# Four changes of order in a two-layer decoder: RG-LRU queues, PSUM banks of the last out-projection, and the weights of the attention layer's output

## The chip, the cores and the metric

The kernel runs on one core of a Trainium2 chip. Its time is device microseconds of one execution; the time before is the median of three runs, 1180.68 us (1180.13 to 1182.38). The five engines are called PE (TensorE, matmuls), DVE (VectorE), ACT (ScalarE), POOL (GpSimd) and SP (SyncE, which here issues the DMAs). Each works off its own queue in the order in which the program was laid out for it.

## The reference

The input is 1024 tokens of 1024 channels in float32. Two pre-norm residual layers follow each other, then a last RMS norm.

```python
def lru_mixer(h, w_in, conv_w, conv_b, wa, ba, wx, bx, a_param, w_out):
    u = h @ w_in
    xb, gate = u[..., :LRU_WIDTH], u[..., LRU_WIDTH:]          # 1536 each
    xc = causal_depthwise_conv(xb, conv_w, conv_b)             # 4 taps
    r = sigmoid(block_diag_linear(xc, wa, ba))                 # 12 blocks of 128
    i = sigmoid(block_diag_linear(xc, wx, bx))
    log_a = -8.0 * r * softplus(-a_param)
    a = exp(log_a)
    bterm = sqrt(-expm1(2.0 * log_a)) * (i * xc)
    hs = scan(a, bterm)                    # h_t = a_t * h_(t-1) + bterm_t
    return (hs * silu(gate)) @ w_out

def fox_mixer(h, w_in, b_f, w_out):        # 16 heads of 64, causal
    q, k, v, gate, f_logit = split(h @ w_in)
    cum = cumsum(log_sigmoid(f_logit + b_f))
    p = softmax(causal(q k' / 8 + cum_q - cum_k))
    return (p v * silu(gate)) @ w_out

for i in (0, 1):
    x = x + (lru_mixer, fox_mixer)[i](rms_norm(x, norm_g[i]), ...)
return rms_norm(x, final_g)
```

## The kernel before

Channels lie on the 128 partitions, tokens run along the free dimension, in two halves of 512. Every float32 matrix is split into a rounded part and a remainder (names ending in `h` and `l`), and each product is three matmuls: high by high, weight remainder by high, weight by remainder (lines 111 to 113). Weights come from memory into a tile `wf` (three buffers), ACT casts the rounded part (`wh`, line 75), POOL subtracts for the remainder (`wl`, line 86); `wh` and `wl` have four buffers each. PSUM has eight banks: two single ones of tag `g`, two of tag `O`, and two pairs of tag `S`.

The program is written as ordinary nested loops and generators. A scheduler simulates the engines with its own estimate of every duration, and puts an instruction on its engine's queue when it is ready in that simulation; among ready ones the one that was written (traced) first goes first. `tc.issue_after(ins)` adds an order to this: every instruction traced in its block that runs on the engine of `ins` comes behind `ins` in the queue. It makes nobody wait for a result.

The first layer goes over 12 blocks of 128 channels (`n`). Each makes 48 matmuls `ups` (the convolution's input), 48 `gps` (the gate branch) and 12 `gate` (the block-diagonal products). `conv(n)` scales `ups` into `us` on DVE (line 260), which frees the pair of banks, makes the first tap on ACT (`xc`, line 261) and three more on DVE (line 264), and splits the result (`xch` on ACT, `xcl` on DVE). `gates(n)` has four products in the two banks of tag `O`, each freed by a tanh on ACT (line 285): two into `th`, two into `ti`; `state[n]["last"]` is the last of them. `recur(n)` makes two more functions and a square on ACT (lines 310 to 312), a product on DVE (313), a square root on ACT (315, with a table load before it and one before the next tanh), products and the scan on DVE (314, 316, 317). `silu` and `outputs` finish the block (294 to 296, 325, and the split into `yh` and `yl`). In iteration `n` the order of the trace is: half of `ups` of `n`, gates of `n - 1`, outputs of `n - 2` (behind `last` already), the other half of `ups`, convolution of `n`, fill, `gps` of `n - 1`, silu and recurrence of `n - 1`, fill. Fill is the out-projection of two finished blocks (`project_out`): 16 units of six matmuls (8 row blocks `db` by two halves), each in one bank of tag `g` and added to the residual `x` on DVE (line 350). Eight units are taken in each iteration from 3 on, so eight of the last sixteen are left when the loop ends; these are drained after the last `gps`, ahead of the last recurrence. The last two blocks' out-projection (lines 429 to 431) uses the pairs of tag `S`.

The second layer goes over 16 heads. For each, `run` works off a string in which digits step the attention's generators and a dot steps the fill and a side list. From head 13 on the fill is `partial`: the output projection of the first six pairs of heads, 8 row blocks by two token halves, 18 matmuls per unit in a bank of tag `g`, added to the first layer's residual, which is loaded and stored again. Before it `load_y` loads the two halves' `y` and splits them (ACT and DVE). The side list of head 14 is `late`: it loads the weights of the last pair of heads and casts them (`woh`, `wol`) into the tiles of the keys and queries, which are free when head 15's loads (lines 566 to 574) have read them; then it loads the `y` of pair 6. Lines 655 and 656 are the logits for the softmax statistics, 660 and 663 their maximum (DVE) and exponentials (ACT); 722 and 723 are the logits for the weights, 756 and 757 the products with the values.

Of the kernel before, what the change touches and what calls it, by code (L numbers as in the profile page):

```python
# [2 lines left out]

# [1 line left out]

# [6 lines left out]
F32 = mybir.dt.float32  # L12
# [3 lines left out]
ALU = mybir.AluOpType  # L16
# [22 lines left out]
def trunk(ctx: ExitStack, tc: tile.TileContext, xt, w0, wg, wo0, pc, gn, w1, wv, wf, bf, wo1, out):  # L39
# [59 lines left out]
    def weights(src, parts=wpool, lo_eng=nc.gpsimd):  # L99

        for k in range(0, src.shape[1], 4):
            n = min(4, src.shape[1] - k)
            yield from split_weights([(src[:, k : k + n], slice(0, P))], (n, P), nc.scalar, lo_eng, parts)
# [13 lines left out]
    def drain(gen):  # L117
        for _ in gen:
            pass
# [44 lines left out]
    with ExitStack() as l0:  # L164
# [92 lines left out]
        def conv(n, ups):  # L257
            us, xc = long("us"), long("xc", bufs=2)
            for pt, cs in zip(ups, halves if len(ups) == 2 else (slice(0, SEQ),)):
                nc.vector.tensor_tensor(us[:, cs], pt, rs[:, cs], ALU.mult)  # L260
            nc.scalar.activation(xc, us, AF.Identity, bias=cb[:, n : n + 1], scale=cw[3][:, n : n + 1])
            for d in range(1, 4):
                w_ = cw[3 - d][:, n : n + 1]
                nc.vector.scalar_tensor_tensor(xc[:, d:], us[:, : SEQ - d], w_, xc[:, d:], ALU.mult, ALU.add)
            xh, xl = long("xch", F32R), long("xcl", F32R)
            to_hi(xh, xc, nc.scalar)
            to_lo(xl, xc, xh, nc.vector)
            wt = wpool.tile([P, 4, P], F32, tag="wf", name="wgf", bufs=3)[:, :2]
            nc.sync.dma_start(wt, wg[n])
            wgh = tmp.tile([P, 2, P], F32R, tag="wgh", name="wgh")  # L270
            wgl = tmp.tile([P, 2, P], F32R, tag="wgl", name="wgl")
            to_hi(wgh, wt, nc.vector)
            to_lo(wgl, wt, wgh, nc.vector)
            state[n] = dict(xc=xc, x=(xh, xl), w=(wgh, wgl))
# [24 lines left out]
        def recur(n, parts=(slice(0, SEQ),)):  # L299
            s = state[n]  # L300
            a, t = long("a", bufs=2), long("m2")
            s["a"] = a
            old = 0.0
            for cs in parts:
                th, ti = (z[:, cs] for z in s["t"])
                a_, t_, xc = a[:, cs], t[:, cs], s["xc"][:, cs]

                nc.scalar.activation(t_, th, AF.Tanh, bias=c2[:, n : n + 1], scale=c2[:, n : n + 1])  # L310
                nc.scalar.activation(a_, th, AF.Exp, bias=nc2[:, n : n + 1], scale=nc2[:, n : n + 1])
                nc.scalar.activation(th, a_, AF.Square)
                nc.vector.scalar_tensor_tensor(t_, th, 1.0, t_, ALU.add, ALU.mult)
                nc.vector.scalar_tensor_tensor(ti, ti, 1.0, xc, ALU.add, ALU.mult)
                nc.scalar.activation(t_, t_, AF.Sqrt, scale=1.0 / 16.0)
                nc.vector.tensor_tensor(ti, ti, t_, ALU.mult)
                nc.vector.tensor_tensor_scan(a_, a_, ti, old, ALU.mult, ALU.add)
                old = a[:, cs.stop - 1 : cs.stop]

        def outputs(n, parts=(slice(0, SEQ),), gate=itertools.repeat(None)):  # L320
            s = state.pop(n)
            y = tuple(ypool.tile([P, SEQ], F32R, tag=z, name=z) for z in ("yh", "yl"))
            for cs, _ in zip(parts, gate):
                a_ = s["a"][:, cs]
                nc.vector.tensor_tensor(a_, a_, s["sg"][:, cs], ALU.mult)
                yh, yl = (z[:, cs] for z in y)
                to_hi(yh, a_, nc.scalar)
                to_lo(yl, a_, yh, nc.vector if len(parts) > 1 else nc.gpsimd)
            ys.append(y)

        def out_weights(g, d0):

            wt = wpool.tile([P, 4, P], F32, tag="wf", name="wf", bufs=3)
            for j in range(2):
                nc.sync.dma_start(wt[:, 2 * j : 2 * j + 2], wo0[d0 + j, :, 2 * g : 2 * g + 2])
            hi = wpool.tile([P, 4, P], F32R, tag="wh", name="wh")
            lo = wpool.tile([P, 4, P], F32R, tag="wl", name="wl")
            to_hi(hi, wt, nc.scalar)
            to_lo(lo, wt, hi, nc.gpsimd)
            return [[(hi[:, 2 * j + i], lo[:, 2 * j + i]) for i in range(2)] for j in range(2)]  # L340

        def project_out(g):

            for d0 in range(0, KT, 2):
                for db, w in enumerate(out_weights(g, d0), d0):
                    for h, cs in enumerate(halves):
                        pt = ps.tile([P, HALF], F32, tag="g", name="ops")
                        gemm(pt, zip(w, [tuple(z[:, cs] for z in p) for p in ys[2 * g : 2 * g + 2]]))
                        x = xs[h][db]
                        nc.vector.tensor_tensor(x, x, pt, ALU.add)  # L350
                        yield
# [11 lines left out]
        for n in range(NB):  # L363
            wu = first[0] if n == 0 else list(weights(w0[n]))
            if n == 1:
                ups = both = [ps.tile([P, HALF], F32, tag="g", name="ups") for h in range(2)]
            else:
                ups = two_banks("ups")
                both = [ups.rearrange("p a b -> p (a b)")]
                ups = [ups[:, h] for h in range(2)]  # L370
            product(ups[0], 0, wu)
            if n == 0:
                gps = held[0] = two_banks("gps")
                product(gps[:, 0], 0, first[1])
                for _ in zip(split_x(1), square_x(1)):
                    pass
                done = rms_row(sums[0], rs[:, :HALF])[1]
            else:
                gates(n - 1)
                if n > 1:  # L380
                    with tc.issue_after(state[n - 1]["last"].ins):
                        outputs(n - 2)
            product(ups[1], 1, wu)
            if n == 0:
                product(gps[:, 1], 1, first[1])
                rms_row(sums[1], rs[:, HALF:])
                with tc.issue_after(done.ins):
                    softplus()
            conv(n, both)
            if n % 2 and n > 1:  # L390
                fill = itertools.chain(fill, project_out((n - 3) // 2))
            take(fill, 4)
            if n > 1:
                wn = list(weights(w0[NB + n - 1]))
                gps = held[n - 1] = two_banks("gps")
                for h in range(2):
                    product(gps[:, h], h, wn)
            if n:
                drain(silu(state[n - 1], held.pop(n - 1)))
                recur(n - 1)  # L400
            take(fill, 4)
        gates(NB - 1)
        wn = list(weights(w0[2 * NB - 1]))
# [1 line left out]
        for h in range(2):  # L405
            product(gps[:, h], h, wn)
        outputs(NB - 2)
        drain(fill)
        recur(NB - 1, halves)
        outputs(NB - 1, halves, silu(state[NB - 1], gps, halves))  # L410
# [53 lines left out]
    with ExitStack() as l1:  # L464
# [344 lines left out]

        def partial():  # L810

            for db in range(KT):
                w = list(weights(wo1[db, :, :6]))
                for c in range(2):
                    x = at.tile([P, HALF], F32, tag="xp", name="xp", bufs=3)
                    nc.sync.dma_start(x, x1d[c, :, db])
                    pt = ps.tile([P, HALF], F32, tag="g", name="ops1")
                    yield from gemm_steps(pt, zip(w, y1[c]))
                    nc.vector.tensor_tensor(x, x, pt, ALU.add)
                    nc.sync.dma_start(x1d[c, :, db], x)  # L820

        def final(c, q):

# [57 lines left out]

        def late():

            for half in range(2):
                wh, wl = (kqpool.tile([P, 8, P], F32R, tag=f"qk{p}{half}", name=f"wo{p}") for p in "hl")
                for b in range(2):
                    wt = wpool.tile([P, 4, P], F32, tag="wf", name="wf", bufs=3)
                    for d in range(2):
                        nc.sync.dma_start(wt[:, 2 * d : 2 * d + 2], wo1[half * 4 + b * 2 + d, :, 6:8])
                    sl = slice(4 * b, 4 * b + 4)  # L890
                    to_hi(wh[:, sl], wt, nc.scalar)
                    to_lo(wl[:, sl], wt, wh[:, sl], nc.gpsimd)
                    yield
                late_w.extend([(wh[:, 2 * d + k], wl[:, 2 * d + k]) for k in range(2)] for d in range(4))
            for c in range(2):
                load_y(c, [6])
                yield
# [125 lines left out]
```

## Time and profile before

| | |
|---|---|
| median of three runs | 1180.68 us |
| profiled execution | 1183.53 us |
| its span | 1181.8 us |
| mean granted TensorE clock | 0.985 |
| first layer | to about 465 us |
| second layer | from about 465 us |

The profile is of one execution. Engine rows give the start, the duration, the engine, the line, the operation, output and inputs, shapes and count; in brackets stands how long the engine had been idle and what ended that. Window rows give the length of a stretch and, for each engine, busy time and instructions, then the granted clock and the DMA share. Busy times of PE come from modelled ends of matmuls, so the distance from one start to the next says more than a duration.

### The profile page before, as it was taken

The page shows a single profiled execution, that of the slowest core. Times are in us where ns is not written, and L with a number is a line of the kernel's source. Part 1 is how long each engine was busy: PE and PEld are TensorE (multiplying, and loading weights), DVE is VectorE, ACT ScalarE, POOL GpSimd, SP SyncE. Part 2 cuts the span into 40 slices and gives each one's busy share as a digit, 9 for nine tenths or more (in the row PEclk, how much of TensorE's full clock was granted, in tenths as well). Part 3 has the DMA queues.
Part 4 walks back from the last instruction along what each step waited for, and adds up shares of the span by engine and source line. Part 5 has one row for each costly group of instructions (what it writes and reads, how often), then busy time and mean ns, then how long its engine had stood idle before and what let it go on. Part 6 is the DMA issues. An engine that isn't in the chain of part 4 may idle for free.

```text
span 1181.8 us, 15783 instructions
## 1 busy us (share of the span) xinstructions
PE 1142.6 (97%) x5653; PEld 954.9 (81%) x5653; DVE 808.6 (68%) x1237; ACT 589.0 (50%) x1010; POOL 415.2 (35%) x370
## 2 busy tenths in 40 slices
PE   9998999999999998999999999999999999998996
PEld 7786788888888875878888988889888898787896
DVE  7588855777565877865777646776567765575666
ACT  8386354354553644464554545554455444435343
POOL 1233342333342422442343332433434334144345
PEclk9999999999999999999999999999999999999996
DMA  6111111111211114143343414433234332756434
GB/s 207 50 40 40 50 54 41 49 58 32 58 40 55 54 62 160 52 117 90 82 125 82 109 54 99 114 77 99 64 90 108 90 82 59 197 148 198 143 115 142
DMA packets 63277, 105.94 MB, mean 90 GB/s; under 512 B 8856, under 2 KB 27928, under 8 KB 63200
## 3 DMA queue, kind: packets, MB, share of 16 engines
q1 hardware_dynamic: 63200, 104.95, 31.7%
q8 instruction: 44, 0.72, 0.2%
q14 instruction: 33, 0.27, 0.1%
HBM read 63.30 MB, written 16.45 MB: 67 GB/s over the span
## 4 chain that ended last, share of the span: by engine, by line
PE 79%; DVE 10%; issue 3%; ACT 3%; DMA 3%; POOL 1%; SPq 1%; DVEq 0%; ACTq 0%; POOLq 0%
PE gps L113 10%; PE gps L112 10%; PE gps L111 10%; PE ops L111 5%; PE ops L112 5%; PE ops L113 5%; PE ups L113 3%; PE ups L111 3%; PE ST L722 3%; PE ups L112 3%; PE O L757 3%; PE ST L723 3%; PE S L656 3%; PE S L655 3%; PE O L756 3%
## 5 line engine op out<-in xcount | busy, mean ns | idle before, releaser
L86 POOL TENSOR_TENSOR wl<-wf,wh 128x512 fp32r<-128x512 f32 (+2 forms) x154 | 227.6, 1485 | 457.2 <-ACT wh L75 420.5
L113 PE MATMUL gps<-hl,wh 128*128 128x512 f32 x576 | 227.8, 396 | 2.5 <-DVE hl L86 2.5
L111 PE MATMUL gps<-hh,wh 128*128 128x512 f32 x576 | 227.5, 395 | 2.0 <-ACT hh L75 2.0
L112 PE MATMUL gps<-hh,wl 128*128 128x512 f32 x576 | 227.5, 395 | 0.0
L663 ACT ACTIVATE S<-S,st 128x128 f32<-128x128 f32 (+7 forms) x128 | 91.5, 715 | 149.1 <-DVE st L660 147.1
L75 ACT CAST wh<-wf 128x512 fp32r<-128x512 f32 (+2 forms) x156 | 93.7, 606 | 105.8 <-issue 27.2
L113 PEld LDWEIGHTS gps<-hl,wh 128*128 128x128 f32 x576 | 108.9, 189 | 26.8 <-DVE hl L86 3.0
L111 PEld LDWEIGHTS gps<-hh,wh 128*128 128x128 f32 x576 | 109.1, 189 | 23.7 <-ACT hh L75 2.5
L112 PEld LDWEIGHTS gps<-hh,wl 128*128 128x128 f32 x576 | 109.0, 189 | 21.2 <-POOL wl L86 0.3
L81 DVE CAST ph<-p 128x512 fp32r<-128x512 f32 (+2 forms) x130 | 80.4, 630 | 65.6 <-POOL p L736 38.4
L86 DVE TENSOR_TENSOR pl<-p,ph 128x512 fp32r<-128x512 f32 (+2 forms) x130 | 117.0, 919 | 2.0
L660 DVE CUSTOM_DVE_ANT_0 S<-S,mask 128x128 f32<-128x128 f32 (+7 forms) x128 | 96.8, 759 | 19.5 <-PE S L656 18.7
L736 POOL TENSOR_SCALAR_AFFINE_SELECT p<-p 128x128 f32<-128x128 f32 (+1 forms) x128 | 48.9, 400 | 127.3 <-ACT p L731 75.8
L350 DVE TENSOR_TENSOR x<-x,ops 128x512 f32<-128x512 f32 x80 | 53.6, 681 | 41.2 <-PE ops L113 40.9
L111 PE MATMUL ups<-hh,wh 128*128 128x512 f32 x192 | 76.5, 399 | 2.6 <-DVE us L260 1.9
L112 PE MATMUL ups<-hh,wl 128*128 128x512 f32 x192 | 75.5, 393 | 0.7 <-POOL wl L86 0.7
L113 PE MATMUL ups<-hl,wh 128*128 128x512 f32 x192 | 75.9, 395 | 0.2
L519 PE MATMUL vps<-wh,hh 128*128 128x256 f32 (+1 forms) x256 | 73.0, 286 | 1.6 <-DVE fz L531 1.6
L728 ACT ACTIVATE p<-ST 128x512 f32<-128x512 f32 (+1 forms) x68 | 52.9, 787 | 40.3 <-PE ST L723 35.4
L521 PE MATMUL vps<-wl,hh 128*128 128x256 f32 (+1 forms) x256 | 72.8, 286 | 0.0
L520 PE MATMUL vps<-wh,hl 128*128 128x256 f32 (+1 forms) x256 | 72.2, 283 | 0.0
L655 PE MATMUL S<-T,U 128*128 128x256 f32 (+2 forms) x192 | 67.5, 354 | 1.7 <-ACT S L663 1.6
(196 smaller groups left out, 2604.2 us busy)
## 6 DMA issues: line engine op xcount, KB each, us to landing
wf<-in_w SPq DMA_DIRECT2D x100, 256.0 KB
wf<-in_wo SPq DMA_DIRECT2D x64, 128.0 KB
T<-qkh SPq DMA_DIRECT2D x28, 256.0 KB
U<-qkh SPq DMA_DIRECT2D x28, 256.0 KB
x<-in_xt SPq DMA_DIRECT2D x16, 256.0 KB
x1d<-x SPq DMA_DIRECT2D x16, 256.0 KB
wf<-in_wv SPq DMA_DIRECT2D x16, 256.0 KB
xp<-x1d SPq DMA_DIRECT2D x16, 256.0 KB
```

The costliest lines, as they stand in the source:

```text
L75: nc.scalar.copy(hi, src)
L81: eng.tensor_copy(hi, src)
L86: return eng.tensor_tensor(lo, src, f32(hi), ALU.subtract)
L111: nc.tensor.matmul(o, wh, xh[:, cs], start=i == 0, stop=False)
L112: nc.tensor.matmul(o, wl, xh[:, cs], start=False, stop=False)
L113: nc.tensor.matmul(o, wh, xl[:, cs], start=False, stop=i == len(pairs) - 1)
L519: nc.tensor.matmul(pt, xh, wh, start=k == 0, stop=False)
L520: nc.tensor.matmul(pt, xl, wh, start=False, stop=False)
L521: nc.tensor.matmul(pt, xh, wl, start=False, stop=k == KT - 1)
L655: nc.tensor.matmul(S[:, lo_:hi_], U[s][:, 0, qs], T[s][:, 0, lo_:hi_], start=True, stop=False)
L660: nc.vector.tensor_tensor_reduce(S[:, :n], S[:, :n], mask[:, SEQ - n :], -1.0, -NEG, ALU.add, ALU.min, accum_out=m)
L663: nc.scalar.activation(S[:, :n], S[:, :n], AF.Exp, bias=f32(m), scale=-1.0, accum_out=sums[:, i : i + 1])
```

## The change

It has four edits. None adds or removes arithmetic or a transfer.

1. `conv(n)` (for `n` of 1 and more) and `recur(n - 1)` in the loop are traced inside `issue_after` of the last tanh of block `n - 1`: their ACT instructions (the first tap, the rounded split; the functions, the square and the root) come behind all four tanh of that block in ACT's queue. The last block's recurrence, after the loop, is not wrapped.
2. In the eight units drained after the loop, those of odd row blocks take a pair of banks of tag `S` in place of two single ones of tag `g`.
3. `partial` takes its first four units as (row block 0, half 0), (1, 0), (0, 1), (1, 1); before it was (0, 0), (0, 1), (1, 0), (1, 1). Two row blocks' weights are then held at once.
4. `late` begins with four empty steps, so that everything in it is traced four dots later.

```diff
@@ project_out
             for d0 in range(0, KT, 2):
                 for db, w in enumerate(out_weights(g, d0), d0):
+                    wide = two_banks("ops") if held is None and db % 2 else None
                     for h, cs in enumerate(halves):
-                        pt = ps.tile([P, HALF], F32, tag="g", name="ops")
+                        if wide is None:
+                            pt = ps.tile([P, HALF], F32, tag="g", name="ops")
+                        else:
+                            pt = wide[:, h]
@@ the loop over n
-            conv(n, both)
+            with tc.issue_after(state[n - 1]["last"].ins) if n else nullcontext():
+                conv(n, both)
...
             if n:
                 drain(silu(state[n - 1], held.pop(n - 1)))
-                recur(n - 1)
+                with tc.issue_after(state[n - 1]["last"].ins):
+                    recur(n - 1)
...
         outputs(NB - 2)
+        held = None
         drain(fill)
@@ partial
-            for db in range(KT):
-                w = list(weights(wo1[db, :, :6]))
-                for c in range(2):
-                    x = at.tile([P, HALF], F32, tag="xp", name="xp", bufs=3)
-                    nc.sync.dma_start(x, x1d[c, :, db])
-                    pt = ps.tile([P, HALF], F32, tag="g", name="ops1")
-                    yield from gemm_steps(pt, zip(w, y1[c]))
-                    nc.vector.tensor_tensor(x, x, pt, ALU.add)
-                    nc.sync.dma_start(x1d[c, :, db], x)
+            ws = {}
+            for db, c in [(0, 0), (1, 0), (0, 1), (1, 1)] + [(db, c) for db in range(2, KT) for c in range(2)]:
+                if db not in ws:
+                    ws[db] = list(weights(wo1[db, :, :6]))
+                x = at.tile([P, HALF], F32, tag="xp", name="xp", bufs=3)
+                nc.sync.dma_start(x, x1d[c, :, db])
+                pt = ps.tile([P, HALF], F32, tag="g", name="ops1")
+                yield from gemm_steps(pt, zip(ws[db], y1[c]))
+                nc.vector.tensor_tensor(x, x, pt, ALU.add)
+                nc.sync.dma_start(x1d[c, :, db], x)
@@ late
+            yield from itertools.repeat(None, 4)
             for half in range(2):
```

More of the change, by code (lines that the diff above doesn't have):

```diff
@@ L1 @@
 import itertools
-from contextlib import ExitStack
+from contextlib import ExitStack, nullcontext
 import numpy as np
```

## The prediction

> **What bounds the kernel now.** I read the page's busy times first, then the table of windows stage by stage, then the timelines of the engines around each stretch in which TensorE (PE) loses time.
>
> ```profile
> PE 1142.6 (97%) x5653; PEld 954.9 (81%) x5653; DVE 808.6 (68%) x1237; ACT 589.0 (50%) x1010; POOL 415.2 (35%) x370
> ```
>
> ```profile
> core 0: us, PE busy (x) PEld busy (x) DVE busy (x) ACT busy (x) POOL busy (x), PEclk, DMA share, GB/s
> 60.00:97.00 37.00, 37.00 (x162) 29.84 (x160) 33.31 (x25) 27.41 (x31) 12.47 (x7) 1.00 0.17 54
> 97.00:116.00 19.00, 14.06 (x52) 9.85 (x51) 15.56 (x12) 16.60 (x18) 6.28 (x3) 0.91 0.05 13
> 116.00:420.00 304.00, 303.61 (x1315) 246.72 (x1314) 204.58 (x191) 149.87 (x176) 103.63 (x59) 1.00 0.16 48
> 420.00:430.00 10.00, 7.89 (x33) 5.79 (x33) 9.92 (x11) 1.91 (x4) 4.74 (x3) 1.00 0.25 79
> 1020.00:1032.00 12.00, 9.11 (x36) 7.20 (x35) 7.08 (x13) 6.34 (x13) 1.97 (x2) 0.86 0.67 186
> 1060.00:1077.00 17.00, 13.67 (x56) 10.63 (x55) 7.06 (x12) 7.41 (x15) 9.15 (x9) 0.90 0.81 221
> ```
>
> PE is the bound: it is busy 97% of the span, and the change removes no matmul. So only its pauses, and what the clock loses behind them, can be won. From 116 to 420 us there is nothing to win (303.61 of 304.00 busy); 1315 matmuls in 304.00 us are 0.231 us each, my unit below. The four other windows are the places that the four edits touch. From 97 to 116, 52 matmuls should take 12.0 us and take 19.0: **7.0 lost**. From 420 to 430, 33 should take 7.6: **2.4 lost**. From 1020 to 1032 PE pauses 2.89, and from 1060 to 1077 it is idle 17.00 - 13.67 = **3.3**.
>
> **The change part by part.**
>
> *Convolution and root behind the tanh.* In the stretch from 97 ScalarE (ACT) works off its queue in an order that starves PE:
>
> ```profile
> 94.16 0.69 ACT L285 ACTIVATE th<-gate,hba 128x512 f32<-128x512 f32 x1
> 97.50 1.24 ACT L261 ACTIVATE xc<-us,pct 128x1024 f32<-128x1024 f32 x1 [2.66 <-DVE us L260]
> 98.65 0.67 ACT L285 ACTIVATE th<-gate,hba 128x512 f32<-128x512 f32 x1
> 106.73 1.28 ACT L285 ACT_TABLE_LOAD   x1
> 108.02 0.69 ACT L285 ACTIVATE ti<-gate,hbx 128x512 f32<-128x512 f32 x1
> ```
>
> ```profile
> 99.37 0.50 PE L111 MATMUL gate<-xch,wgh 128*128 128x512 f32 x1 [2.01 <-ACT th L285]
> 108.76 0.50 PE L111 MATMUL gate<-xch,wgh 128*128 128x512 f32 x1 [2.21 <-ACT ti L285]
> 109.86 0.63 PE L111 MATMUL ops<-yh,wh 128*128 128x512 f32 x1
> ```
>
> The convolution of block 3 (xc at 97.50) stands between the two th of block 2 and waits 2.66 us for DVE; the second th, its bank full, waits behind it, and PE waits for the bank. At 108.76 the same happens with the last ti, behind a root and a table load. With the edges all four tanh go first, and neither pause can arise in this way: this is the 7.0, with the slow matmuls that follow (0.63 at 109.86). On the clock: behind the pause of 2.21 the rows are 0.63 long. [...]
>
> The price is paid earlier, where the convolution now runs ahead because ACT has nothing to do:
>
> ```profile
> 57.90 1.25 ACT L261 ACTIVATE xc<-us,pct 128x1024 f32<-128x1024 f32 x1 [0.29 <-DVE us L260]
> 68.74 1.04 ACT L75 CAST xch<-xc 128x1024 fp32r<-128x1024 f32 x1
> 69.68 0.69 ACT L285 ACTIVATE ti<-gate,hbx 128x512 f32<-128x512 f32 x1
> ```
>
> ```profile
> 59.18 4.83 DVE L264 SCALAR_TENSOR_TENSOR xc<-us,pct,xc 128x1023 f32<-128x1023 f32 x3 [0.18 <-ACT xc L261]
> 64.11 1.23 DVE L260 TENSOR_TENSOR us<-ups,rs 128x1024 f32<-128x1024 f32 x1
> 68.30 1.22 DVE L313 SCALAR_TENSOR_TENSOR m<-th,m 128x1024 f32<-128x1024 f32 x1 [2.96 <-ACT th L312]
> 70.10 1.22 DVE L86 TENSOR_TENSOR xcl<-xc,xch 128x1024 fp32r<-128x1024 f32 x1
> 72.77 1.23 DVE L316 TENSOR_TENSOR ti<-ti,m 128x1024 f32<-128x1024 f32 x1 [0.32 <-ACT m L315]
> 77.22 1.26 DVE L264 SCALAR_TENSOR_TENSOR xc<-us,pct,xc 128x1023 f32<-128x1023 f32 x1
> ```
>
> ```profile
> 67.68 0.39 PE L113 MATMUL gate<-xcl,wgh 128*128 128x512 f32 x1
> 73.43 0.39 PE L111 MATMUL gate<-xch,wgh 128*128 128x512 f32 x1
> ```
>
> Block 1's xc runs at 57.90, before block 0's tanh; it must now wait for their last. PE issues block 0's last gate product at 67.68, so, nothing else standing before it, that ti ends at about 68.9 and xc at 70.1. Queued behind the waiting xc is xch alone, but DVE needs it: three taps (4.83 at 59.18, or three of the single tap at 77.22, 3.8; I take 3.9) end at 74.0, m of the recurrence takes 1.2, xch 1.04 beside it, xcl 1.22, so block 1's gates start near 76.5 instead of 73.43. And us of block 2, which frees the two banks for ups of block 3, moves from 64.11 to 76.4. PE's other product, gps of block 1, has three matmuls left at 73.43, so without these gates it ends at 74.1. So I expect a **new pause of 2.4 us near 74**. Behind it the clock costs between nothing (the pause of 2.01) and 10 matmuls at 0.2 more (2.0, the pause of 2.21); I take 1.3. DVE, busy 33.31 of 37.00, has some 6 us less done by 70, which the 11 us of a later ups hide as long as its banks are free by 103. Sum: -7.0 + 2.4 + 1.3 = **-3.3**, bounds -7.0 (no new pause) and +8 (below).
>
> In the later blocks:
>
> ```profile
> 236.93 1.25 ACT L310 ACTIVATE m<-th,c 128x1024 f32<-128x1024 f32 x1
> 242.79 1.04 ACT L75 CAST yh<-a 128x1024 fp32r<-128x1024 f32 x1
> ```
>
> ```profile
> 247.61 3.20 DVE L317 TENSOR_TENSOR_SCAN a<-a,ti 128x1024 f32<-128x1024 f32 x1
> 261.73 2.24 DVE L325 TENSOR_TENSOR a<-a,sg 128x1024 f32<-128x1024 f32 x1
> ```
>
> The recurrence's first steps run between th and ti; behind the last ti (yh at 242.79 follows it) they start at most 5.9 later, and the scan ends by 256.7, where its reader starts at 261.73. xc, waiting for less, comes sooner. Cover 5.0 us; cost 0. Were it gone, each microsecond late would be one on POOL's yl and then on the products, which have eight units queued ahead.
>
> *Four banks for the last chain's products.*
>
> ```profile
> 424.09 0.67 DVE L350 TENSOR_TENSOR x<-x,ops 128x512 f32<-128x512 f32 x1
> ```
>
> ```profile
> 424.81 0.50 PE L111 MATMUL ops<-yh,wh 128*128 128x512 f32 x1 [1.35 <-DVE x L350]
> ```
>
> The wait is on an eviction that DVE reaches only at 424.09, behind the last recurrence. But the first two products after gps are of an even row block (db = 4) and stay in the old two banks; only db 5 and 7 go wide. So the pause named by the row stays: **0**, bounds -2.4 (the chain before it starts sooner, or db 5 goes first) and +1 (the tail's own products want the same banks).
>
> *Second half's y further back.*
>
> ```profile
> 1027.06 0.68 DVE L626 SCALAR_TENSOR_TENSOR sg<-sg,gps 128x512 f32<-128x512 f32 x1
> ```
>
> ```profile
> 1027.80 0.80 PE L111 MATMUL ops<-yhh,wh 128*128 128x512 f32 x1 [2.89 <-DVE sg L626]
> ```
>
> The second unit starts 0.06 us after sg gives its bank back, whatever y it reads. The new second unit, row block 1 of the first half, needs the same bank. The loads and casts of y keep their place on SP, ACT and DVE. Two row blocks' weights now hold all four wh and wl buffers until the third unit ends; the next pair's casts have the fourth unit (18 matmuls, 4.2 us) to hide under. **0**, bounds -4.2 (2.89 and six slow matmuls at 0.2) and +2 (those casts late).
>
> *Late weights' casts.*
>
> ```profile
> 1064.25 0.62 ACT L75 CAST woh<-wf 128x512 fp32r<-128x512 f32 x1 [7.16 <-DMA T<-qkh]
> 1067.57 0.76 ACT L663 ACTIVATE S<-S,st 128x640 f32<-128x640 f32 x1
> ```
>
> ```profile
> 1061.76 0.08 DVE L660 DVE_READ_ACCUMULATOR2_ANT st<- 128x1 fp32r x1
> ```
>
> ```profile
> 1068.50 0.50 PE L722 MATMUL ST<-U,T 128*128 128x512 f32 x1 [1.67 <-ACT S L663]
> 1071.14 0.49 PE L655 MATMUL S<-T,U 128*128 128x512 f32 x1 [1.56 <-ACT S L663]
> ```
>
> The cast into the old key and query tiles blocks ACT for 7.16 us, till head 15's loads have read them. The softmax step ready at 1061.84 runs at 1067.57, behind two casts, and PE pauses 1.67 and 1.56. Four steps later in the trace, the casts come after all four softmax steps of that head in rank. The loads on SP that they wait for do not move, so the first cast may still stand at the head; but if the softmax only passes the second cast it runs at 1064.9, 2.7 sooner, more than each pause. I take both: **-3.2**, bounds 0 (order kept) and -5 (the clock too). The two y loads at the end of this list move back with it; their result is read only in the last products, after the attention: 0.
>
> Sum: -3.3 + 0 + 0 - 3.2 = -6.5. The profiled execution took 1183.53 (span 1181.8 and 1.7 around it), 2.85 above the median of the three runs; I carry the difference over: 1180.68 - 6.5 = **1174.2 us**.
>
> **Rivals.**
>
> *All four places are cleared*: no new pause at 74, the order before 424 shifts, the bank at 1027 comes sooner. -7.0 - 2.4 - 4.2 - 5.0 = -18.6, 1162 us. For it: each edit lies at one of the pauses. Against it: two of the four waits are on things that the edits do not touch.
>
> *Nothing lands*: the pauses return under other names, since DVE is as full as ACT is blocked, and the casts stay where they are: 1178.5 to 1183, near 1180.5. For it speaks 33.31 of 37.00 on DVE.
>
> *Slower: DVE starves PE in the first blocks.* The 6 us of taps and us that DVE did by 65.3 move into its full stretch. If there the recurrence's m, the product with the root (72.77) and the scan (1.2 + 1.2 + 3.2 = 5.6) come before us of block 2, the pause near 74 grows from 2.4 to 8.0, plus 2.0 of clock: 10.0 against the 7.0 won, 1183.7; if block 2 repeats it, 1193. It decides once the new pauses exceed 7.0 (with the casts' 3.2, 10.2). Against it: the convolution is traced ahead of the recurrence and goes first where both are ready.
>
> **How the numbers follow.** A measurement can tell 0.2%, 2.4 us, from no change. Forecast with its bounds (1169 to 1178) 0.53; all cleared 0.13; nothing lands 0.13; slower 0.21. Faster 0.66, same 0.13, slower 0.21. The range of 1165 to 1185 leaves out half of the all-cleared case and the repeated starvation, 0.17 in all.
>
> **What would show it.** Right: block 1's xc at about 69, after two ti; a PE pause near 74; the four tanh of every block adjacent, and no PE wait for ACT between 95 and 112; the wait for x L350 near 420 still there; the wait for sg L626 still there; the step of 640 columns ahead of the second woh. Wrong: pauses above 7 us in all before 90; a wait for yl or us after 116; a wait for wl in the partial products; woh still ahead of the 640-column step.

## The result and the profile after

| | before | after |
|---|---|---|
| median of six runs each, same chip | 1181.64 us (1180.13 to 1183.33) | 1190.05 us (1188.37 to 1192.34) |
| profiled execution, its span | 1183.53, 1181.8 us | 1189.03, 1187.1 us |
| mean granted clock | 0.985 | 0.978 |

The change makes the kernel slower: ratio 1.0074, 95% interval 1.0061 to 1.0086. The forecast was 1174.2 us with a range of 1165 to 1185, so sign and range were both missed. The spans of the two profiles differ by 5.3 us only, because the profile of before lies 1.9 above the median of its runs and that of after 1.0 below.

The busy times of after, in the same order of engines:

```profile
PE 1148.0 (97%) x5653; PEld 960.3 (81%) x5653; DVE 793.1 (67%) x1237; ACT 590.0 (50%) x1010; POOL 417.8 (35%) x370
```

The number of instructions is the same on every engine; TensorE's (PE's) busy time has grown by 5.4, about as much as the span. Where, the windows of after say (the columns are those of the prediction's table):

```profile
60.00:74.00 14.00, 14.00 (x62) 11.43 (x62) 5.12 (x6) 7.79 (x10) 2.65 (x3) 1.00 0.16 47
74.00:90.00 16.00, 12.94 (x49) 9.86 (x48) 13.13 (x9) 7.93 (x10) 3.94 (x2) 0.89 0.11 34
90.00:121.00 31.00, 31.00 (x136) 25.24 (x135) 25.71 (x19) 22.73 (x26) 14.49 (x7) 1.00 0.17 47
121.00:133.00 12.00, 8.53 (x25) 6.03 (x24) 11.08 (x10) 6.77 (x9) 1.89 (x2) 0.72 0.14 44
...
60.00:140.00 80.00, 73.46 (x297) 58.24 (x297) 62.00 (x50) 50.29 (x58) 24.85 (x13) 0.94 0.16 46
```

A full-rate matmul took 0.231 us in before (1315 in the 304.00 us from 116 on, at a granted clock of 1.00), so a stretch has lost its length less 0.231 times its matmuls. From 90 to 121 nothing is lost any more: the pauses that before had between 97 and 116 are gone. But 74 to 90 loses 16 - 49 x 0.231 = 4.7, and 121 to 133 loses 12 - 25 x 0.231 = 6.2. Over 60 to 140 after loses 80 - 297 x 0.231 = 11.4. The same window of before:

```profile
60.00:140.00 80.00, 74.67 (x313) 58.63 (x312) 71.41 (x57) 54.15 (x61) 28.85 (x15) 0.98 0.15 46
```

80 - 313 x 0.231 = 7.7. This count, "lost in 60 to 140", is used for every kernel below. (A stretch without a pause, 90 to 121 here, comes out at -0.4, so the count is good to about half a microsecond.) The two new losses are three waits on PE:

```profile
75.69 0.50 PE L111 MATMUL gate<-xch,wgh 128*128 128x512 f32 x1 [0.76 <-ACT xch L75]
79.19 0.47 PE L111 MATMUL ups<-hh,wh 128*128 128x512 f32 x1 [2.31 <-DVE us L260]
125.13 0.80 PE L111 MATMUL gate<-xch,wgh 128*128 128x512 f32 x1 [3.47 <-ACT xch L75]
125.73 0.63 PE L112 MATMUL gate<-xch,wgl 128*128 128x512 f32 x1
```

The rest of the loss is time at half clock behind them (a granted clock of 0.50 in 80 to 82 and in 125 to 129 us, and 0.63 for a row, as in the last one). Elsewhere three things are to be seen. The wait for x at the drained units is still there. The last two blocks' out-projection has two new waits for x, at 466.33 (1.37, not shown) and 471.85, and its last wait stands 8.5 us later than in before (463.38). The wait for sg has shrunk from 2.89 to 0.65:

```profile
430.73 0.50 PE L111 MATMUL ops<-yh,wh 128*128 128x512 f32 x1 [1.81 <-DVE x L355]
471.85 0.50 PE L438 MATMUL ops<-yh,wh 128*128 128x512 f32 x1 [2.29 <-DVE x L456]
1031.86 0.50 PE L111 MATMUL ops<-yhh,wh 128*128 128x512 f32 x1 [0.65 <-DVE sg L635]
```

### The profile page after: what moved, and what is told of

It reads as the page before. It is cut to its first block, busy times and chain, and to the rows that moved or that the text cites. A ratio compares the mean times of both kernels' runs of the same rounds, so it can differ in the third digit from the quotient of the medians.

```text
span 1187.1 us, 15780 instructions
## 1 busy us (share of the span) xinstructions
PE 1148.0 (97%) x5653; PEld 960.3 (81%) x5653; DVE 793.1 (67%) x1237; ACT 590.0 (50%) x1010; POOL 417.8 (35%) x370
## 4 chain that ended last, share of the span: by engine, by line
PE 85%; DVE 7%; DMA 3%; ACT 2%; issue 1%; SPq 1%; POOL 0%; DVEq 0%; ACTq 0%; POOLq 0%
PE gps L113 10%; PE gps L111 10%; PE gps L112 10%; PE ops L112 5%; PE ops L111 5%; PE ops L113 5%; PE ups L111 4%; PE ups L113 4%; PE ups L112 4%; PE O L766 3%; PE ST L731 3%; PE O L765 3%; PE S L665 3%; PE S L664 3%; PE ST L732 3%; PE vps L528 2%
## 5 line engine op out<-in xcount | busy, mean ns | idle before, releaser
L86 POOL TENSOR_TENSOR wl<-wf,wh 128x512 fp32r<-128x512 f32 (+2 forms) x154 | 233.2, 1522 | 464.8 <-ACT wh L75 424.7
L86 DVE TENSOR_TENSOR pl<-p,ph 128x512 fp32r<-128x512 f32 (+2 forms) x130 | 119.6, 939 | 2.1
L112 PE MATMUL ups<-hh,wl 128*128 128x512 f32 x192 | 76.5, 398 | 0.0
L731 PE MATMUL ST<-U,T 128*128 128x512 f32 (+1 forms) x198 | 67.1, 346 | 3.5 <-ACT S L672 3.5
```

Of the source, the lines that this page charges most:

```text
L86: return eng.tensor_tensor(lo, src, f32(hi), ALU.subtract)
L112: nc.tensor.matmul(o, wl, xh[:, cs], start=False, stop=False)
L731: nc.tensor.matmul(A[:, jj, :n], T[s][:, 0, ks], U[s][:, 0, q0:end], start=True, stop=False)
```

## Why the first blocks lose: three queues of after

ACT, DVE and POOL of after, around the two losses:

```profile
69.37 1.23 ACT L261 ACTIVATE xc<-us,pct 128x1024 f32<-128x1024 f32 x1
74.59 1.05 ACT L75 CAST xch<-xc 128x1024 fp32r<-128x1024 f32 x1 [0.26 <-DVE xc L264]
113.02 1.03 ACT L295 ACTIVATE sg<-gps 128x1024 f32<-128x1024 f32 x1 [2.43 <-DVE gps L294]
113.94 1.26 ACT L285 ACTIVATE ti<-gate,hbx 128x512 f32<-128x512 f32 x2
115.08 1.05 ACT L75 CAST yh<-a 128x1024 fp32r<-128x1024 f32 x1
116.01 1.26 ACT L261 ACTIVATE xc<-us,pct 128x1024 f32<-128x1024 f32 x1
124.04 1.04 ACT L75 CAST xch<-xc 128x1024 fp32r<-128x1024 f32 x1 [3.03 <-DVE xc L264]
```

```profile
70.64 3.92 DVE L264 SCALAR_TENSOR_TENSOR xc<-us,pct,xc 128x1023 f32<-128x1023 f32 x3
77.84 1.21 DVE L260 TENSOR_TENSOR us<-ups,rs 128x1024 f32<-128x1024 f32 x1
95.60 6.06 DVE L264 SCALAR_TENSOR_TENSOR xc<-us,pct,xc 128x1023 f32<-128x1023 f32 x3 [0.86 <-ACT xc L261]
117.31 6.70 DVE L264 SCALAR_TENSOR_TENSOR xc<-us,pct,xc 128x1023 f32<-128x1023 f32 x3 [0.21 <-ACT xc L261]
```

```profile
94.51 2.51 POOL L86 TENSOR_TENSOR yl<-a,yh 128x1024 fp32r<-128x1024 f32 x1 [2.65 <-ACT yh L75]
116.21 3.15 POOL L86 TENSOR_TENSOR yl<-a,yh 128x1024 fp32r<-128x1024 f32 x1 [5.45 <-ACT yh L75]
120.12 1.49 POOL L86 TENSOR_TENSOR wl<-wf,wh 128x512 fp32r<-128x512 f32 x1 [0.76 <-ACT wh L75]
```

Block 1's xc runs at 69.37 instead of 57.90. In the kernel before, the second block's convolution ran ahead of the first gates, and its xch lay ready when PE came to its gates. With the edge each block is a chain: last gate product, tanh, (yh,) xc, three taps, xch, next gates. PE has to fill that chain with other products, and how many stand there is fixed by the order that the scheduler worked out with its own estimates. The table sets the chain, from the end of the gates before to the end of xch, against these products (0.231 us each). The last five rows are kernels of the experiments below.

| kernel, block | chain, us | products in front | their time, us | difference | wait for xch |
|---|---|---|---|---|---|
| after, 1 | 7.0 | 27 | 6.2 | 0.8 | 0.76 |
| after, 2 | 10.2 | 56 | 12.9 | none | none |
| after, 3 | 13.1 | 41 | 9.5 | 3.6 | 3.47 |
| both edges from n = 2, 2 | 10.2 | 56 | 12.9 | none | none |
| both edges from n = 2, 3 | 10.6 | 54 | 12.5 | none | none |
| both edges from n = 3, 3 | 11.2 | 47 | 10.9 | 0.3 | 0.28 |
| one edge, 1 | 12.3 | 27 | 6.2 | 6.1 | 6.07 |
| edit 1, y behind the convolution, 2 | 7.0 | 5 | 1.2 | 5.8 | 5.80 |

In every row the wait is the difference, to within 0.15. The serial chain that the edge makes costs no wait in the three rows with 54 or 56 products in front. In after, block 3 has 13 fewer than in the kernel with both edges from n = 2: 13 of `ups` were already taken at 107.6. Why the scheduler orders them so was not looked into. The wait of 2.31 at 79.19 is another one: `ups` of block 3 needs the banks that us of block 2 frees, and that us runs at 77.84 instead of 64.11, behind block 1's taps.

Two things lengthen block 3's chain. The silu (sg) stands in front of its last two tanh and waits 2.43 for DVE. And the taps take 6.70 instead of 3.92, as they take 6.06 in block 2; in both POOL works on yl and wl beside them. It is busy for 3.59 us beside block 2's taps and for 3.54 beside block 3's, against 1.11 beside block 1's (wl alone), and none beside block 3's in before (98.78 to 102.70), which take 3.92 as well. That the overlap makes them slow is read from these rows, and how it does was not shown; the run that moves yl away from block 2's taps is among the experiments below.

## The experiments

Each kernel was timed against the kernel before on the same chip. "Lost" is what PE loses in 60 to 140 us, by the count above, from one profile each. (The expectations call it excess and count with a slightly shorter matmul, so before has 8.3 there.)

| kernel | median us | ratio to before, 95% | lost |
|---|---|---|---|
| before | 1181.6 to 1183.1 | 1 | 7.7 |
| after | 1190.05 | 1.0074 (1.0061 to 1.0086) | 11.4 |
| edit 1 alone | 1186.51 | 1.0036 (1.0022 to 1.0050) | 12.5 |
| edit 2 alone | 1182.67 | 1.0001 (0.9990 to 1.0013) | 7.7 |
| edit 3 alone | 1182.83 | 1.0002 (0.9993 to 1.0012) | 7.0 |
| edit 4 alone | 1184.06 | 1.0015 (1.0004 to 1.0027) | 7.9 |
| edits 1 and 2 | 1188.44 | 1.0040 (1.0023 to 1.0057) | 11.4 |
| convolution's edges alone | 1203.62 | 1.0180 (1.0158 to 1.0201) | 18.6 |
| root's edges alone | 1176.55 | 0.9951 (0.9932 to 0.9970) | 1.7 |
| one edge: block 1's convolution | 1193.58 | 1.0096 (1.0078 to 1.0114) | 13.9 |
| both edges from n = 2 | 1175.36 | 0.9941 (0.9920 to 0.9962) | 1.7 |
| both edges from n = 3 | 1174.99 | 0.9941 (0.9919 to 0.9964) | 0.5 |
| edit 1, y behind the convolution | 1206.10 | 1.0198 (1.0175 to 1.0221) | 19.5 |
| whole change, edges from n = 3 | 1177.27 | 0.9957 (0.9942 to 0.9972) | 1.5 |
| whole change without one edge | 1180.57 | 0.9983 (0.9973 to 0.9993) | 4.5 |

**The four edits, each alone.** Edit 1 alone:

```diff
-            conv(n, both)
+            with tc.issue_after(state[n - 1]["last"].ins) if n else nullcontext():
+                conv(n, both)
...
-                recur(n - 1)
+                with tc.issue_after(state[n - 1]["last"].ins) if n else nullcontext():
+                    recur(n - 1)
```

> Edit 1 alone. Theory A (the convolution behind the tanh starves TensorE in the first blocks): 3 to 5 us slower than before; pauses of about 3 us near 75 and 3.5 us near 121 as with all four edits, the two pauses at 99 and 109 gone. Theory B (the loss is the drained units in four banks): within 2 us of before or faster, since the pauses won (7.0) and new (9.5 with the slow clock) nearly balance only in the profile. The wait for x L350 near 425 stays in both.

Measured: +4.3 us, as theory A had it. The pauses of after come back in the same places (0.76 at 75.40, 2.29 at 78.90 for us, 3.48 at 124.72 for xch), and 12.5 is lost in 60 to 140. About half of the whole loss is here.

Edit 2 alone:

```diff
+                    wide = two_banks("ops") if held is None and db % 2 else None
...
+                            pt = wide[:, h]
...
+        held = None
         drain(fill)
```

> Edit 2 alone. Theory A: 1 to 3 us slower, from longer pauses between 450 and 480 (the norm of the first half starts later, because the eight units run ahead of it and their evictions sit in front of it on VectorE). Theory B: the whole 8 us. A third reading, that the tail of the profile after only shifted with the first blocks: no change, 0 plus or minus 1.5.

Measured: no difference. PE of this kernel still waits at the two even units, by the same amount as before (1.35 and 0.76 there), and has new waits in the last two blocks' out-projection (the last row; 1.35 at 461.35 is the other):

```profile
424.65 0.50 PE L111 MATMUL ops<-yh,wh 128*128 128x512 f32 x1 [1.36 <-DVE x L354]
427.06 0.50 PE L111 MATMUL ops<-yh,wh 128*128 128x512 f32 x1 [0.76 <-DVE x L354]
466.87 0.50 PE L434 MATMUL ops<-yh,wh 128*128 128x512 f32 x1 [1.46 <-DVE x L452]
```

In before the last such wait is one of 0.43, at 463.38. The 3.5 us are made up behind it: the next layer's wait for hl is 0.53 instead of 2.54, and its first softmax logits start at 512.76 instead of 513.45.

Edit 3 alone:

```diff
-            for db in range(KT):
...
+            for db, c in [(0, 0), (1, 0), (0, 1), (1, 1)] + [(db, c) for db in range(2, KT) for c in range(2)]:
```

> Edit 3 alone. If the order of the units is what shortened the wait for sg near 1027 (2.89 before, 0.65 with all four edits): 2 to 4 us faster, that wait under 1 us. If it was the late weights' loads that moved: 0 plus or minus 1.5, and the wait still near 2.9.

Measured: no difference. PE's two waits of this kernel, the second where before has 1.67:

```profile
1028.12 0.51 PE L111 MATMUL ops<-yhh,wh 128*128 128x512 f32 x1 [0.47 <-DVE sg L626]
...
1069.87 0.78 PE L722 MATMUL ST<-U,T 128*128 128x512 f32 x1 [2.90 <-ACT S L663]
```

The wait for sg falls from 2.89 to 0.47, and the wait for S grows by 1.23. The wait for sg lies between 0.46 and 2.54 in the other kernels that have neither edit 3 nor edit 4, so its size says little about the edit, and neither reading of the expectation is borne out: the wait shrank and no time was won.

Edit 4 alone:

```diff
         def late():
+            yield from itertools.repeat(None, 4)
             for half in range(2):
```

> Edit 4 alone. If moving the late weights' loads out of the way of the y loads shortened the wait for sg near 1027: 2 to 4 us faster, that wait under 1 us. Otherwise 0 plus or minus 1.5. In both the casts keep their place ahead of the 640-column softmax step, with some 7 us of wait for the loads of T and two pauses of TensorE near 1068 of 1 to 2 us each.

Measured: +1.8 us (0.5 to 3.2). ACT, DVE and PE of this kernel, and the load on SyncE (SP):

```profile
1063.56 0.62 ACT L75 CAST woh<-wf 128x512 fp32r<-128x512 f32 x1 [6.87 <-DMA T<-qkh]
1067.26 0.76 ACT L663 ACTIVATE S<-S,st 128x640 f32<-128x640 f32 x1
1083.59 0.62 ACT L75 CAST yhh<-y 128x512 fp32r<-128x512 f32 x1 [3.54 <-DMA y<-y1d]
```

```profile
1084.24 0.69 DVE L86 TENSOR_TENSOR yhl<-y,yhh 128x512 fp32r<-128x512 f32 x1 [3.38 <-ACT yhh L75]
1084.85 0.29 DVE L660 CUSTOM_DVE_ANT_0 S<-S,mask 128x128 f32<-128x128 f32 x1
```

```profile
1080.55 0.28 PE L655 MATMUL S<-T,U 128*128 128x256 f32 x1
1085.80 0.44 PE L655 MATMUL S<-T,U 128*128 128x384 f32 x1 [1.24 <-ACT S L663]
```

```profile
1080.61 0.33 SPq L807 DMA_DIRECT2D y<-y1d  x1
```

The first reading expected a gain, and 0 plus or minus 1.5 is missed by a little. The wait for sg is 0.28 in this kernel, and no time is won by that. The casts of woh have not moved in the queue: ACT is blocked for 6.87 (7.16 before), and the 640-column step still runs behind two of them. What moved is the y load at the end of the list, from 1066.48 to 1080.61. Its cast blocks ACT for 3.54, DVE's subtraction waits for the cast, and behind that stands the maximum of head 15's first logits, which PE had issued at 1080.55. PE then waits for the next banks. From 1060 to 1115 PE is idle for 6.0 us in this profile, for 3.6 in that of before. A wait of this kind is in the profile after too. No run moved the casts without the y loads, so that the y loads are the whole of the 1.8 is read from the trace and not tested.

**Which edge, and which block.** The convolution's edges alone, and the root's alone (each is one of the two `with` lines of edit 1):

> The convolution alone behind the gates' tanh, the root left free as in the kernel before. Theory A (the chain of convolution is now serial: last tanh, xc, three taps, cast of xch, next gates): the new pauses of the run with both edges come back, 2.3 for us near 79 and 3.5 for xch near 125, excess in 60 to 140 us about 11 to 13 against 8.3 before; 1184.5 to 1188. Rival R (the root's place costs it, since the root and its table load now stand behind): no pause over 1.5 at those two places, 1180 to 1183.

> The root's group alone behind the gates' tanh, the convolution free as in the kernel before. Theory A: the taps and xch keep the order of before, so no new pause for xch; a switch of the activation table inside a pair of tanh's is gone, so part of the 8.3 lost in 60 to 140 us goes; 1178 to 1182. Rival R (the root's place costs): pauses for xch or us near 79 and 125, 1184.5 to 1188.

The two parts have opposite signs: +1.8% and -0.5%. With the root's edges alone PE loses 1.7 in 60 to 140, so 6.0 of the 7.0 that the prediction counted is won; its 1176.55 is better than the 1178 to 1182 that was expected. The convolution's edges without the root's are far worse than with them, and far worse than the 1184.5 to 1188 that was expected: PE waits 6.07 for xch at 83.73, and loses another 9.3 between 140 and 180, where before loses nothing. The next two kernels take both edges out of the first blocks:

```diff
-            with tc.issue_after(state[n - 1]["last"].ins) if n else nullcontext():
+            with tc.issue_after(state[n - 1]["last"].ins) if n > 2 else nullcontext():
                 conv(n, both)
```

(the same for `recur(n - 1)`; then `n > 1`)

> Both edges, but only from the fourth block on (n over 2); the first three blocks as before. Theory A (each block pays for itself): the loss near 75 to 79 (4.2 in the run with both edges) goes, what was lost in 97 to 110 before comes back in part, and the pause for xch near 121 to 125 (3.5 and the slower clock behind it, 6.5 in all) stays; 1183 to 1187. Rival M (it is the first two blocks' delay that makes the fourth one late): both go, excess in 60 to 140 us at 8 or less, 1179 to 1182.

> Both edges from the third block on (n over 1): one block more with edges than in the run from the fourth. Theory M (it is the second block's convolution, pushed from ahead of the first gates to behind them, that makes the later ones late): no pause over 1 for xch in 60 to 140, 1174 to 1177. Rival E (each block without the projection's units to fill TensorE pays for its own edge): a pause of 2 to 6 for xch between 85 and 110, 1178 to 1184.

Both are faster than before by 0.6%, and neither has a pause for xch over 1. Rival M and theory M had that; the first is faster than M's 1179 to 1182. They are the fastest versions found, but their intervals overlap with that of the root's edges alone, so the runs do not show that the convolution's edges add anything to these. In the first, block 3 has its edge; its taps on DVE and its gates on PE:

```profile
103.10 6.57 DVE L264 SCALAR_TENSOR_TENSOR xc<-us,pct,xc 128x1023 f32<-128x1023 f32 x3 [0.46 <-ACT xc L261]
```

```profile
110.81 0.50 PE L111 MATMUL gate<-xch,wgh 128*128 128x512 f32 x1 [0.28 <-ACT xch L75]
```

The taps are as slow as in after, yet PE waits only 0.28: block 3's chain is 11.2 long here and not 13.1, and 47 products stand in front of its end and not 41. So the edge of its own block does not make the pause at 125; the edges of the first blocks change what stands there. One edge alone was then added to the kernel before, and taken out of the whole change:

```diff
-            conv(n, both)
+            with tc.issue_after(state[n - 1]["last"].ins) if n == 1 else nullcontext():
+                conv(n, both)
```

> The kernel before with one single edge: the convolution of the second block (n = 1) behind the first gates' tanh, nothing else changed. Theory M: a pause for xch or us between 70 and 90 of 2 to 6 and a later one again; slower, 1184 to 1200 (the run with all convolutions' edges and no root's gave 1203.6). Rival F (one edge alone is made up for by the convolutions behind it, which are free): 1179 to 1183.5.

```diff
-            with tc.issue_after(state[n - 1]["last"].ins) if n else nullcontext():
+            with tc.issue_after(state[n - 1]["last"].ins) if n > 1 else nullcontext():
                 conv(n, both)
```

> The whole change with one single edge taken out: the convolution of the second block (n = 1) is free, every other edge and edit stays. Theory M (that one convolution's place carries the loss of the first blocks): excess in 60 to 140 us at 3 or less, and about the time of the run with the edges from the third block on plus 2 for the other edits: 1176 to 1180. Rival E (the root's edge in that block, or the later convolutions', carry it too): 1182 to 1190.

One edge on one convolution makes the kernel before slower by 11.6 us; without it the whole change is 0.17% faster than before. The first is inside theory M's range, though of the two waits that M named only the first is there. The second, 1180.57 with 4.5 lost, lies between the two ranges: that edge carries most of the loss, not all. What is left holds a wait of 2.00 for wl at 124.97, with half clock behind it (0.50 in 126 to 128). ACT, DVE and PE of the kernel with this one edge:

```profile
70.16 1.23 ACT L261 ACTIVATE xc<-us,pct 128x1024 f32<-128x1024 f32 x1
80.70 1.04 ACT L75 CAST xch<-xc 128x1024 fp32r<-128x1024 f32 x1 [1.28 <-DVE xc L264]
```

```profile
73.80 1.23 DVE L316 TENSOR_TENSOR ti<-ti,m 128x1024 f32<-128x1024 f32 x1 [1.08 <-ACT m L315]
74.94 2.30 DVE L264 SCALAR_TENSOR_TENSOR xc<-us,pct,xc 128x1022 f32<-128x1022 f32 x1
77.16 2.28 DVE L317 TENSOR_TENSOR_SCAN a<-a,ti 128x1024 f32<-128x1024 f32 x1
79.36 1.25 DVE L264 SCALAR_TENSOR_TENSOR xc<-us,pct,xc 128x1021 f32<-128x1021 f32 x1
```

```profile
81.80 0.80 PE L111 MATMUL gate<-xch,wgh 128*128 128x512 f32 x1 [6.07 <-ACT xch L75]
```

Without the root's edge the recurrence's product and scan come between the taps, xch is 6.1 later than in after, and PE waits 6.07. The same wait opens the losses of the kernel with the convolution's edges alone.

**POOL beside the taps.** Edit 1 with the outputs behind the convolution's xcl:

```diff
-                if n > 1:
-                    with tc.issue_after(state[n - 1]["last"].ins):
-                        outputs(n - 2)
...
                 conv(n, both)
+            if n > 1:
+                with tc.issue_after(state[n]["xl"].ins):
+                    outputs(n - 2)
```

> Both edges in every block, and outputs (the product with the gate, ACT's cast yh, POOL's yl) moved from ahead of the convolution to behind its xcl. Theory P (POOL's yl beside DVE's taps slows them from 3.9 to 6.1 and 6.7, and this makes the pause for xch near 125): three taps take 3.9 to 4.3 in each of the first blocks, the pause near 125 falls under 1, and 4 to 6 of the 6.5 lost there are gone; 1179 to 1183. Rival Q (the taps are slow for another reason, or the chain is late without them): the taps stay at 6 or the pause for xch stays above 2.5; 1185 to 1188.

DVE and PE of this kernel:

```profile
94.26 3.91 DVE L264 SCALAR_TENSOR_TENSOR xc<-us,pct,xc 128x1023 f32<-128x1023 f32 x3
```

```profile
99.30 0.80 PE L111 MATMUL gate<-xch,wgh 128*128 128x512 f32 x1 [5.80 <-ACT xch L75]
```

The half about the taps is right: with yl moved away block 2's take 3.91 instead of 6.06. The half about the time is wrong: 1206.1, the slowest of all. The scheduler put only 5 products between block 1's gates and block 2's here, where after has 56, so the same chain, though shorter, costs 5.80. The order changed with the edit, so this run does not say what the slow taps cost in after. An estimate from after's own rows: block 3's chain less 2.8 would be 10.3 long, and with 41 products in front the wait would be 0.8 instead of 3.47. That was not tested.

**What else is in the loss.**

The first two edits together, and the whole change with `n > 2` in both edges:

> The edges on convolution and root in all blocks and the four banks, no other edit. Theory I (the part of the loss that the four single runs do not give, about 2, is the four banks beside the edges, in the drained units and the norm behind them): 1188 to 1190, excess between 420 and 520 us larger by about 2 than with the edges alone. Rival N (they add up): 1186 to 1187.5.

> The whole change, but both edges only from the fourth block on (n over 2): the first three blocks as before. Theory L (the edges cost where the convolution loses its lead over the gates in the first blocks, and the rest of the change costs what it did in single runs): excess in 60 to 140 us at 3 or less against 11.9 with the whole change, and 1175.0 of the run without the other three edits plus their single costs 0.2, 0.2 and 1.8: 1176 to 1179. Rival S (the loss belongs to the four banks and the late casts once the edges are there): 1183 to 1190.

Edits 1 and 2 together give 1.0040 against 1.0036 for edit 1: the runs show no loss of their own between them, though the two intervals leave room for the 2 us of theory I, and the time, 1188.44, lies in its range. In the profile the last wait of the out-projection's tail stands at 472.24, and at 468.33 with edit 1 alone. With the edges from n = 3 on, the three other edits raise the ratio from 0.9941 to 0.9957, intervals overlapping, in keeping with 0.2, 0.2 and 1.8 us alone. The four single runs sum to 1.0054; the whole change is at 1.0074. The difference, 2.4 us, is no larger than what the five intervals put together allow (about 0.27%, 3 us), so the runs do not show that anything is left over.

## Why the prediction was wrong

*The 7.0 of 97 to 116*: right. The pauses are gone in after, the root's edges alone win 6.0 of it, and no table load stands between the tanh of one block there any more.

*The new pause near 74, 2.4 and 1.3 of clock*: the place is right, and the size nearly so, but in part by luck. xc ends at 70.6 (predicted 70.1), and block 1's gates start at 75.69 (predicted 76.5) after a wait of 0.76 only. The larger wait, 2.31, is for us of block 2. The prediction had the time of this us (77.84; predicted 76.4) and no term for it: "the 11 us of a later ups hide" DVE's delay, it says, but `ups` of block 3 stands right behind block 1's gates (at 75.5 in before). This is a second step that failed. The two waits sum to 3.07, and the stretch loses 4.7 instead of 3.7, so the clock took 1.6.

*"In the later blocks ... cost 0"*: this is the step that failed. The cover of 5.0 was read from a block near 240 us, with the fill already flowing, and taken for all blocks behind the first. It was also the recurrence's cover; that of the convolution was not worked out ("xc, waiting for less, comes sooner"). In block 3 the chain is 13.1 us long and has 9.5 us of products in front of its end: a second pause, 3.47 and 2.7 of clock, 6.2 in all. Also left out: DVE's taps beside POOL, 6.06 and 6.70 where 3.9 was taken. The two new losses come to 10.9, clock included, against the 7.0 won. The slower rival had that point right ("once the new pauses exceed 7.0") and priced a repetition at 10, but gave it to the recurrence's work on DVE in front of us of block 2. Of the three instructions that it named only m came there (at 74.48).

*Four banks, 0*: right, and for the reason given: the wait is at an even row block, and stays. The tail's own products do wait more, as the bound of +1 feared (1.35 and 1.46 in the run of this edit alone), and the next layer's start makes up for it.

*Second half's y, 0*: the size is right. The wait for sg was said to stay and did not, but it varies by as much without the edit, and the time of the edit alone shows nothing won.

*Late casts, -3.2*: wrong, +1.8 alone, outside its bounds of 0 and -5. What the bound 0 stood for, order kept, came true: the first cast stays at the head of ACT's queue and still waits for the load of T. These are the casts of after, still ahead of the step, and the later cast of y:

```profile
1067.29 0.62 ACT L75 CAST woh<-wf 128x512 fp32r<-128x512 f32 x1 [6.74 <-DMA T<-qkh]
1071.02 0.76 ACT L672 ACTIVATE S<-S,st 128x640 f32<-128x640 f32 x1
...
1086.70 0.62 ACT L75 CAST yhh<-y 128x512 fp32r<-128x512 f32 x1 [2.07 <-DMA y<-y1d]
```

The step that failed in this term is the sentence on the y loads, "their result is read only in the last products, after the attention: 0". It looked at who reads the result. The wait stands in the queues of ACT and DVE, in front of head 15's softmax (3.54 in the run of this edit alone, 2.07 in the last row here).

*The sum*: these terms as now measured (+3.7 in the first blocks, from the profiles, and +1.8, 0, 0) give 5.5 us. The two profiled executions differ by 5.5, the medians by 8.4; the other 2.9 is how far these two executions lie from their medians, and the profiles cannot place it.

## What to carry to other kernels

An edge that puts work "behind X" must be costed first in the block where that work used to run ahead, and can be left out of that one block (here that alone turned +0.74% into -0.17%). For each wait on a matmul's operand, set the chain from the last product that feeds it against the products that stand between, block by block, and not at one block in mid-stream; and look at the order again after the change, since an edge in one block changed what stood in front of the gates two blocks later. When an edit has two parts, time them apart: here one part alone was 0.5% faster and the other 1.8% slower. When a load is moved, look at the queues in which its cast will wait and not only at who reads the result.

## What the runs showed of the hardware

The granted clock did not follow the length of a pause alone. Windows of before, behind its pause of 2.01 at 99.37, and of the whole change without one edge, behind a wait of 2.00 at 124.97:

```profile
101.00:103.00 2.00, 2.00 (x11) 1.64 (x10) 1.81 (x3) 1.97 (x3) 0.00 (x0) 1.00 0.00 0
```

```profile
126.00:128.00 2.00, 2.00 (x6) 1.52 (x6) 0.59 (x1) 1.64 (x3) 1.14 (x1) 0.50 0.41 124
```

The first keeps the full clock (1.00), the second falls to half (0.50). After's pauses of 2.31 and 3.47 are both followed by half clock (0.50 in 80 to 82 and in 125 to 129), and cost 1.6 and 2.7 us beyond their own length. So a pause of 2.00 was followed by half clock here and one of 2.01 was not; what else decides was not shown.
